# Part of group 1's B/C and of group 2's x moved into the first phase, four gate pairs moved into the first scan stage

## The chip, the cores and the metric

One core of one Trainium2 chip. The metric is device time in microseconds of one execution, as a median over runs. The core has a matrix engine (TensorE, PE, with its weight loads, PEld), a vector engine (VectorE, DVE), a scalar engine (ScalarE, ACT), GpSimd (POOL), and SyncE (SP), whose queue issues most transfers; transfers run on 16 DMA engines. Each engine executes its own list of instructions in order and waits on semaphores for the others.

## The reference, cut to what matters

One layer of a diffusion backbone: 256 latent tokens x and 256 context tokens ctx, model width 2048.

```python
hx = modulate(rmsnorm(x, norm_mix), sh1, sc1)      # sh1, sc1 from silu(c) @ w_mod + b_mod
proj = h @ w_in                                    # for x and for ctx
z, xbc, dt_raw, glu, gates = split(proj, [4096, 10240, 10368, 14464])
xbc = silu(dwconv_seq(xbc, conv_w, conv_b))        # width 5, centred
xs, bm, cm = split(xbc, [4096, 5120])              # 64 heads of 64; 8 groups of state 128
y = ssd_chunked(forward) + flip(ssd_chunked(flipped)) # x starts from the end states of ctx
y_a = rmsnorm((y + d_skip * xs) * silu(z), ssm_norm) @ w_proj_a
u, v = split(glu, 2); cf = silu(layernorm(cf_conv(u * sigmoid(v))))
g_a, g_b = split(gates, 2)
x = x + g1 * ((sigmoid(g_a) * y_a + sigmoid(g_b) * (cf @ w_proj_b)) @ w_out)
x = x + g2 * swiglu(modulate(rmsnorm(x, norm_ffn), sh2, sc2)) ; out = rmsnorm(x, norm_final)
```

All inputs are float32. The scan of a group needs its own x, B, C and dt; z is needed after the scan; the gates only near the end of the first sub-layer.

## The kernel before, in words

Every large product is made from two float32r halves: a weight tile w (float32, 128 x up to 1024) is cast to wh by ACT (line 114), and DVE makes the rest wl = w - wh (line 115); the activations hx are kept as a high and a low half in the same way. The 512 columns of hx are 256 latent and 256 context tokens. `mm_unit` (132) multiplies one unit of weights: up to four row blocks (128 rows of the model width each, 16 in all) by 256 columns, that is two parts of 128 columns. A wide part (1 in the list `wide`) has three 128x512 matmuls per row block, for latent and context tokens; a narrow part (0) has one 128x512 and one 128x256, for latent tokens alone. A weight tile lives in w32 (6 buffers, filled from SP's queue, line 107), then in wh and wl (4 each). Accumulators are PSUM tiles `acc`, four in all, so two pairs of parts.

**First phase (358 to 517).** The modulation vectors sh1 and sc1 come from 64 units of w_mod that PE multiplies with silu(c) (`mod_units`, 400, line 413), and they are needed before hx of a row block can be made (429 to 440). So the product with w_in starts before hx is complete: the row blocks are taken in blocks (`BLOCKS`), and for each block a list of `pairs` of columns is multiplied: dt, the x tiles of groups 0 and 1 (four x pairs of 256 columns) and B and C of group 0. The partial sums are added in SBUF after each block (line 509). Between the pairs of one block stand the mod_units of the next block. With the last block the sums are complete: they get the conv and SiLU (`conv`, 279: ACT, four DVE taps, ACT), and `dt_chain` (301) makes the decay tables in small steps and sends cs_d and ec_d to DRAM.

**Scan stages 1 to 8 (796 to 824).** Stage s runs the scan of group s-1 (`ssd`, 584, a generator with 15 steps) between units of w_in: `bcpair` (B and C of group s), `xpair` (x of group s+1), `zpair` (z of an earlier group) and, in stages 7 and 8, `gpair`: five of the 16 gate pairs (256 columns of gates each), which are kept in SBUF in the x tiles' buffers (tag xc, 9 buffers) in the list `early`. Each unit has a nominal duration; `beg` and `end` bound the stretch over which the scan's steps are spread.

**After the scan.** At 826 the gate tiles ga and gb are allocated and the early gates get their sigmoid (832). Then come the GLU pairs (873 to 892), then the remaining gate pairs with the layernorm between them (`layernorm`, 894, nine steps; 922 to 934), then w_proj_b, w_proj_a, w_out, and the FFN. Between their units a `hook` runs steps of `modvec` (519), which reads the other columns of w_mod; `bg(mgen, 108, 226)` sets 108 steps over 226 units.

**What sets the order.** The Python order gives priorities; the list of each engine is fixed when the program is built, by a planner with a cost model that takes the first instruction in this order that is ready by its reckoning. `tc.high_priority(offset=HP)` moves casts, splits and the first phase's additions ahead by 450. A tile of a tag with n buffers waits until the last reader of the tile n before it is done. POOL issues the transfers of `yg_d`, `cs_d` and `ec_d` from its own queue.

## Time and profile before

| | us |
|---|---|
| median of 3 runs (lowest, highest) | 2398.35 (2396.97, 2398.81) |
| the profiled execution's own time | 2399.29 |
| its span, first to last instruction | 2397.6 |
| PE busy | 2337.8 (98%) |
| DVE busy | 1633.7 (68%) |
| ACT busy | 1252.8 (52%) |
| POOL busy | 126.9 (5%) |

The span is cut into stretches from the beginning of the span, given as 30 to 63 us and so on. "Busy" is time in which an instruction of the engine runs; matmuls overlap, so PE's busy time is read with the waits and with the distance from one matmul's start to the next. The granted clock is the share of the 2.4 GHz that TensorE was given. A wait is put down to the semaphore that came last.

### The profile page before, as it was taken

How to read it: one execution, taken by the hardware profiler on the slowest of the kernel's cores; microseconds unless marked ns; L12 is line 12 of the kernel's file. 1: busy time of each engine (PE TensorE's matmuls, PEld its weight loads, DVE VectorE, ACT ScalarE, POOL GpSimd, SP SyncE). 2: the span in 40 equal slices, each digit the busy share in tenths (PEclk: the TensorE clock that was granted, in tenths of full speed). 3: DMA queues.
4: the chain of work that ended last, by engine and by line, in shares of the span. 5: the costliest groups of instructions: out<-in, count | busy, mean ns of one | idle time of the engine just before them, and what ended most of it. 6: DMA issues, size and time to landing. Idle time of an engine off the chain costs nothing.

```text
span 2397.6 us, 34659 instructions
## 1 busy us (share of the span) xinstructions
PE 2337.8 (98%) x13180; PEld 1968.7 (82%) x13180; DVE 1633.7 (68%) x2099; ACT 1252.8 (52%) x1934; POOL 126.9 (5%) x149
## 2 busy tenths in 40 slices
PE   6899999999999999999999999998999999999998
PEld 3668788888888788888888888888888888888888
DVE  4559867676676776889878776767666566655554
ACT  4335766666566675654575444445444444444433
POOL 1000000100000000011300000000000000000000
PEclk9999999999999999999999999999999999999999
DMA  9884545546455566888799987885777677767553
GB/s 276 273 272 135 134 133 150 159 134 159 131 150 162 147 189 192 280 254 284 227 286 300 287 275 249 299 289 169 224 230 222 214 226 225 227 201 247 194 193 115
DMA packets 444848, 510.46 MB, mean 213 GB/s; under 512 B 17944, under 2 KB 391927, under 8 KB 443529
## 3 DMA queue, kind: packets, MB, share of 16 engines
q1 hardware_dynamic: 438904, 488.75, 66.7%
q0 software_dynamic: 5216, 18.41, 2.2%
q8 instruction: 103, 1.69, 0.3%
q10 hardware_dynamic: 560, 1.08, 0.1%
q14 instruction: 65, 0.52, 0.1%
HBM read 499.51 MB, written 8.67 MB: 212 GB/s over the span
## 4 chain that ended last, share of the span: by engine, by line
PE 89%; DMA 5%; DVE 2%; ACT 2%; issue 1%; SPq 1%; DVEq 0%; ACTq 0%
PE acc L152 34%; PE acc L154 18%; PE acc L144 6%; PE acc L145 5%; PE acc L147 5%; PE acc L177 4%; PE acc L174 4%; PE acc L175 4%; DMA w<-in_w_mod_dram 3%; PE acc L156 2%; DMA w<-in_w_in_dram 2%; PE ss L716 1%; PE ss L413 1%; DMA cs<-cs_d 1%; PE ss L686 1%
## 5 line engine op out<-in xcount | busy, mean ns | idle before, releaser
L115 DVE TENSOR_TENSOR wl<-w,wh 128x1024 fp32r<-128x1024 f32 (+3 forms) x702 | 847.1, 1210 | 486.6 <-ACT wh L114 484.4
L114 ACT CAST wh<-w 128x1024 fp32r<-128x1024 f32 (+3 forms) x702 | 717.7, 1024 | 742.2 <-PE acc L152 349.6
L152 PE MATMUL acc<-hx,wh 128*128 128x512 f32 x1556 | 433.0, 397 | 0.0
L152 PE MATMUL acc<-h,wh 128*128 128x512 f32 x1290 | 356.6, 395 | 1.9 <-DVE fe L204 1.9
L152 PEld LDWEIGHTS acc<-hx,wh 128*128 128x128 f32 x1556 | 271.9, 189 | 40.8 <-issue 2.2
L154 PEld LDWEIGHTS acc<-hx,wl 128*128 128x128 f32 x1664 | 254.8, 188 | 37.6 <-DVE wl L115 2.1
L144 PE MATMUL acc<-hx,wh 128*128 128x512 f32 x656 | 266.3, 407 | 3.0 <-ACT wh L114 2.6
L154 PE MATMUL acc<-hx,wl 128*128 128x256 f32 x1664 | 265.1, 281 | 1.4 <-DVE wl L115 1.4
L145 PE MATMUL acc<-hx,wh 128*128 128x512 f32 x656 | 259.2, 395 | 0.2 <-DVE hx L440 0.2
L152 PEld LDWEIGHTS acc<-h,wh 128*128 128x128 f32 x1290 | 225.5, 189 | 34.0 <-DVE fe L204 2.6
L154 PEld LDWEIGHTS acc<-h,wl 128*128 128x128 f32 x1376 | 211.5, 189 | 29.7
L537 DVE SCALAR_TENSOR_TENSOR mac<-w,silc,mac 128x1024 f32<-128x1024 f32 x120 | 154.7, 1289 | 104.7 <-DMA w<-in_w_mod_dram 104.0
L154 PE MATMUL acc<-h,wl 128*128 128x256 f32 x1376 | 219.5, 281 | 0.0
L147 PE MATMUL acc<-hx,wl 128*128 128x512 f32 x656 | 183.2, 392 | 0.0
L144 PEld LDWEIGHTS acc<-hx,wh 128*128 128x128 f32 x656 | 124.2, 189 | 38.1 <-ACT wh L114 8.2
L175 PE MATMUL acc<-wh,hid 128*128 128x512 f32 (+1 forms) x440 | 146.8, 347 | 0.0
L174 PE MATMUL acc<-wh,hid 128*128 128x512 f32 (+1 forms) x440 | 146.8, 347 | 0.0
L145 PEld LDWEIGHTS acc<-hx,wh 128*128 128x128 f32 x656 | 124.3, 190 | 26.3 <-issue 1.4
L147 PEld LDWEIGHTS acc<-hx,wl 128*128 128x128 f32 x656 | 123.3, 188 | 27.2 <-issue 0.7
L152 PE MATMUL acc<-yg,wh 128*128 128x512 f32 x496 | 136.3, 395 | 0.0
L177 PE MATMUL acc<-wl,hid 128*128 128x512 f32 (+1 forms) x440 | 109.5, 347 | 0.0
L667 ACT ACTIVATE cs<-cs,ncs 128x128 f32<-128x128 f32 x256 | 81.6, 390 | 34.6 <-DMA cs<-cs_d 30.9
(331 smaller groups left out, 2795.0 us busy)
## 6 DMA issues: line engine op xcount, KB each, us to landing
w<-in_w_in_dram SPq DMA_DIRECT2D x248, 512.0 KB, 4.5
w<-in_w_mod_dram SPq DMA_DIRECT2D x192, 512.0 KB, 4.8
w<-in_w_ffn_gate_dram SPq DMA_DIRECT2D x88, 512.0 KB, 4.5
w<-in_w_ffn_up_dram SPq DMA_DIRECT2D x88, 512.0 KB, 4.5
w<-in_w_ffn_down_dram SPq DMA_DIRECT2D x88, 512.0 KB, 3.7
w<-in_w_proj_a_dram SPq DMA_DIRECT2D x64, 512.0 KB, 5.0
w<-in_w_in_dram SPq DMA_DIRECT2D x74, 256.0 KB, 3.8
cs<-cs_d SPq DMA_DIRECT2D x32, 512.0 KB, 5.8
```

The costliest lines, as they stand in the source:

```text
L114: A.copy(out=hi[:, :n], in_=t[:, :n])
L115: V.tensor_tensor(out=lo[:, :n], in0=t[:, :n], in1=hi[:, :n].bitcast(F32), op=ALU.subtract)
L144: E.matmul(o, wj(hi, k), act(kofs + k)[:, 0, :ncol], start=kofs + k == kbeg, stop=False)
L145: E.matmul(o, wj(hi, k), act(kofs + k)[:, 1, :ncol], start=False, stop=False)
L147: E.matmul(o, wj(lo, k), act(kofs + k)[:, 0, :ncol], start=False, stop=last and k == nk - 1)
L152: E.matmul(o2, wj(hi, k), act(kofs + k)[:, :, :T], start=kofs + k == kbeg, stop=False)
L154: E.matmul(o[:, :T], wj(lo, k), act(kofs + k)[:, 0, :T], start=False, stop=last and not hold)
L174: E.matmul(o, act(kofs + k)[:, 0, s], hi[:, k], start=kofs + k == 0, stop=False)
L175: E.matmul(o, act(kofs + k)[:, 1, s], hi[:, k], start=False, stop=False)
L177: E.matmul(o, act(kofs + k)[:, 0, s], lo[:, k], start=False, stop=kofs + k == kend - 1)
L537: V.scalar_tensor_tensor(out=ac, in0=wt, scalar=silc[:, k - 1:k], in1=ac, op0=ALU.mult, op1=ALU.add)
L667: A.activation(out=t4[:, r, j], in_=t4[:, r, j], func=AF.Identity, bias=ncs[:, cc, r * 64 + hs + j:r * 64 + hs + j + 1])
```

## The change

Seven blocks become eight: 1, 1, 2, 2, 2, 2, 2, 4. In all blocks but the last the list of pairs has two more: B and C of group 1, and the first x pair of group 2. So after row block 11 their sums stand in SBUF (Bt1, Ct1, xts0[8:10]); the last four row blocks of both follow in scan stage 1, as one unit each, and are added to the sums there. Stage 1 has a new order: the one unit of group 2's first x pair, all of its second x pair, gate pair 0, the one unit of B/C of group 1, gate pairs 1 to 3. The scan's steps start from 20 instead of 8 in nominal time. Stage 7 has gate pair 4, stage 8 gate pairs 5 to 8, so nine instead of five gate pairs are early. An early gate is folded into the tile `sz` (one buffer, which `zpair` and `bcpair` use too) and sent to a DRAM tile eg_d from POOL's queue; it is read back into ga and gb after the scan, and its sigmoid stands after the GLU pairs. Seven gate pairs are left for the stretch of the layernorm, whose nine steps are dealt out as 0, 2, 2, 2, 1, 1, 1; 210 takes the place of 226 in the hook. To make room, xc has 10 buffers, the scan's temporary y shares btok's buffer, and `sta` shares a buffer of h32.

```diff
-BLOCKS = (1, 1, 2, 2, 2, 4, 4)
+BLOCKS = (1, 1, 2, 2, 2, 2, 2, 4)
...
+    eg_d = dpool.tile([P, 2 * KD, T], F32, name="eg_d")
...
-        return pa1.tile([P, 512], F32, tag="xc", name="xc", bufs=9)
+        return pa1.tile([P, 512], F32, tag="xc", name="xc", bufs=10)
...
-        sta = p0.tile([P, 2 * P], F32, name="sta")
+        sta = p0.tile([P, 512], F32, tag="h32", name="h32", bufs=3)
...
-                 ([(OFF_Z + 512, 256)], xts0[4:6], [1, 1]), ([(OFF_Z + 768, 256)], xts0[6:8], [1, 1])]
+                 ([(OFF_Z + 512, 256)], xts0[4:6], [1, 1]), ([(OFF_Z + 768, 256)], xts0[6:8], [1, 1]),
+                 ([(OFF_B + P, P), (OFF_C + P, P)], [Bt1, Ct1], [1, 0]),
+                 ([(OFF_Z + 1024, 256)], xts0[8:10], [1, 1])]
...
+            if last:
+                pairs = pairs[:6]
...
-                    t = ptile([P, 4, P], "y")
+                    t = ptile([P, 4, P], "btok")
...
-        def xpair(g, j):
+        def xpair(g, j, sums=None):
             a = acc2()
-            for k0 in range(0, KD, UK):
+            kb = KD - BLOCKS[-1] if sums else 0
+            for k0 in range(kb, KD, UK):
                 hi, lo = unit_cols(w_in, k0, UK, [(OFF_Z + g * 512 + j * 256, 256)])
-                mm_unit(a, hi, lo, UK, k0, KD, [1, 1], hxa)
+                mm_unit(a, hi, lo, UK, k0, KD, [1, 1], hxa, kbeg=kb)
                 yield
             for i in range(2):
-                xt_[g].append(conv(a[i], 512, g * 4 + 2 * j + i, xct()))
+                o = sums[i] if sums else xct()
+                if sums:
+                    V.tensor_tensor(out=a[i], in0=o, in1=a[i], op=ALU.add)
+                xt_[g].append(conv(a[i], 512, g * 4 + 2 * j + i, o))
...
-            early.append(fold(a, xct().rearrange("p (i t) -> p i t", i=2)))
+            t = fold(a, ptile([P, 2, T], "sz", 1))
+            nc.gpsimd.dma_start(out=eg_d[:, 2 * j:2 * j + 2, :], in_=t)
+            early.append(j)
...
-            gs_ = [(gpair(j), 2.56) for j in {7: [0], 8: [1, 2, 3, 4]}.get(stage, [])]
+            gs_ = [(gpair(j), 2.56) for j in {1: [0, 1, 2, 3], 7: [4], 8: [5, 6, 7, 8]}.get(stage, [])]
...
+            if stage == 1:
+                tasks = [(xpair(2, 0, begun["x"]), 5.12)] + xs_ + gs_[:1] + [(bcpair(1, begun["bc"]), 3.84)] + gs_[1:]
...
-            beg = 8 if stage == 1 else 0
+            beg = 20 if stage == 1 else 0
...
-    for j, t in enumerate(early):
-        A.activation(out=ga[:, 2 * j:2 * j + 2, :], in_=t, func=AF.Sigmoid)
     pas.close()
+    gate = [(ga, gb)[j // 8][:, 2 * (j % 8):2 * (j % 8) + 2, :] for j in range(16)]
+    for j in early:
+        nc.gpsimd.dma_start(out=gate[j], in_=eg_d[:, 2 * j:2 * j + 2, :])
...
-    hook = bg(mgen, 108, 226)
+    hook = bg(mgen, 108, 210)
...
+        for j in early:
+            A.activation(out=gate[j], in_=gate[j], func=AF.Sigmoid)
+        for k in range(0, KD, 2):
+            t = ga[:, k:k + 2, :]
+            V.tensor_tensor(out=t, in0=t, in1=rsta.unsqueeze(1).to_broadcast([P, 2, T]), op=ALU.mult)
+        for j in range(len(early), 16):
+            fold(pair(w_in, OFF_GLU + j * 256, KD, hxa, hook), gate[j])
+            A.activation(out=gate[j], in_=gate[j], func=AF.Sigmoid)
+            for _ in range((0, 2, 2, 2, 1, 1, 1)[j - len(early)]):
+                next(ln, None)
```

`bcpair` is changed as `xpair` is: one unit, then the sums are added to both accumulators ahead of the conv.

## Rows read from the trace of the kernel before

**Rows 1.** The page of the whole execution: its head line, and the busy time of TensorE (PE) in us, its share of the span and its count of instructions.

```profile
span 2397.6 us, 34659 instructions
...
PE 2337.8 (98%) x13180; PEld 1968.7 (82%) x13180; DVE 1633.7 (68%) x2099; ACT 1252.8 (52%) x1934; POOL 126.9 (5%) x149
```

**Rows 2.** Who PE waited for, over the whole span: line and tile of the waiting instruction, what it waited for, and then us in total, times, longest wait in us.

```profile
PE ss L413 <- DMA w<-in_w_mod_dram: 20.3, 12, 12.3
...
PE acc L144 <- ACT wh L114: 2.6, 6, 0.8
...
PE acc L152 <- DVE cfx L945: 2.6, 1, 2.6
...
PE tp L420 <- ACT ev L417: 2.0, 3, 1.0
...
PE acc L154 <- DVE wl L115: 1.4, 1, 1.4
...
PE tp L432 <- DVE sc L421: 0.4, 1, 0.4
```

**Rows 3.** Busy us of each engine, block by block, in the first phase and the first scan stage (columns: stretch, its length, then for PE, weight loads PEld, DVE, ACT and POOL the busy us with the count of instructions, then the granted clock of PE as a share of full speed, the busy share of the DMA engines, and GB/s). The stretches are: row blocks 0 and 1; 2 and 3; 4 and 5; 6 and 7; 8 to 11; 12 to 15 (the last block of the first phase); scan stage 1.

```profile
30.00:63.00 33.00, 29.34 (x237) 17.53 (x235) 18.88 (x44) 14.93 (x36) 0.00 (x0) 1.00 0.92 280
63.00:83.30 20.30, 20.08 (x128) 14.64 (x128) 15.39 (x29) 7.53 (x15) 0.00 (x0) 1.00 0.90 278
83.30:106.00 22.70, 21.91 (x164) 15.52 (x160) 13.21 (x27) 6.25 (x12) 0.00 (x0) 1.00 0.79 237
106.00:142.40 36.40, 31.13 (x228) 20.84 (x224) 19.14 (x38) 9.95 (x19) 0.00 (x0) 0.91 0.87 275
142.40:187.00 44.60, 42.02 (x261) 31.04 (x257) 23.51 (x38) 14.82 (x22) 0.00 (x0) 0.96 0.95 287
187.00:215.60 28.60, 28.60 (x129) 23.75 (x128) 26.68 (x36) 17.13 (x22) 0.00 (x0) 1.00 0.40 113
215.60:302.00 86.40, 84.59 (x433) 66.80 (x432) 78.44 (x119) 60.44 (x119) 5.65 (x6) 1.00 0.48 126
```

**Rows 4.** Who PE waited for between 30 and 187 us, the longest in total (columns as in rows 2; the lines L144, L420 and L432 of rows 2 stand in this answer too, with the same totals).

```profile
PE ss L413 <- DMA w<-in_w_mod_dram: 6.8, 9, 1.6
```

**Rows 5.** PE's timeline at two places in the first phase (start us, duration us, engine, line, operation, output and inputs, shape, count): the first matmul of a slow run of w_in matmuls and the instruction behind that run, and the same a second time.

```profile
116.56 0.78 PE L144 MATMUL acc<-hx,wh 128*128 128x512 f32 x1
...
121.27 0.49 PE L432 MATMUL tp<-ident,xt 128*128 128x128 f32 x3
...
152.52 0.78 PE L144 MATMUL acc<-hx,wh 128*128 128x512 f32 x1
...
154.76 0.39 PE L145 MATMUL acc<-hx,wh 128*128 128x512 f32 x1
```

**Rows 6.** PE's timeline in the first phase (columns as in rows 5): begin and end of the B/C pair over row blocks 4 and 5 (95.03 to 97.22), of an x pair over the same two (101.35 to 104.17), of the B/C pair over row blocks 12 to 15 (200.60 to 204.70) and of an x pair over the same four (210.16 to 215.60).

```profile
95.03 0.50 PE L144 MATMUL acc<-hx,wh 128*128 128x512 f32 x1 [0.79 <-ACT wh L114]
...
97.22 0.40 PE L144 MATMUL acc<-hx,wh 128*128 128x512 f32 x1
...
101.35 0.40 PE L144 MATMUL acc<-hx,wh 128*128 128x512 f32 x1
...
104.17 1.93 PE L413 MATMUL ss<-w,sil 128*32 128x256 f32 x32
...
200.60 0.39 PE L144 MATMUL acc<-hx,wh 128*128 128x512 f32 x1
...
204.70 0.40 PE L144 MATMUL acc<-hx,wh 128*128 128x512 f32 x1
...
210.16 0.39 PE L144 MATMUL acc<-hx,wh 128*128 128x512 f32 x1
...
215.60 0.39 PE L144 MATMUL acc<-hx,wh 128*128 128x512 f32 x1
```

**Rows 7.** What SP's DMA queue waited for between 30 and 187 us, the longest in total (columns as in rows 2).

```profile
SPq L107 <- PE ss L413: 55.4, 37, 5.7
```

**Rows 8.** DVE's timeline at the start: the copy that makes rb, and the first instruction that reads it.

```profile
25.68 0.69 DVE L463 COPY rb<-tp 128x512 f32<-128x512 f32 x1 [0.99 <-PE tp L462]
...
30.47 0.69 DVE L434 TENSOR_TENSOR h<-tp,rb 128x512 f32<-128x512 f32 x1
```

**Rows 9.** Scan stage 1: in DVE's timeline the four taps of one x tile's conv, and the first tap of the B tile of group 1; and line 607, the transposes of the x tiles of group 0 on PE (count, duration in ns as min/median/max, first and last start in us).

```profile
249.85 2.72 DVE L289 SCALAR_TENSOR_TENSOR xc<-xt,vt,xc 128x510 f32<-128x510 f32 x4
252.50 0.74 DVE L289 SCALAR_TENSOR_TENSOR Bt<-acc,vt,Bt 128x508 f32<-128x508 f32 x1
...
L607 PE MATMUL tp<-ident,xc x16: 270/272/273, 245.6 to 260.6; 128*128 128x128 f32 x16
```

**Rows 10.** PE's timeline in the GLU phase: the begin of one unit of a gate or GLU pair (four row blocks, 256 columns), and the begin of the next unit.

```profile
1005.77 1.09 PE L152 MATMUL acc<-hx,wh 128*128 128x512 f32 x4
...
1008.57 1.09 PE L152 MATMUL acc<-hx,wh 128*128 128x512 f32 x4
```

**Rows 11.** The transfers of 256 KB between SBUF and the DRAM tile yg_d, issued from POOL's queue: us from issue to landing.

```profile
DMA to landing us min/median/max: 2.5/4.2/6.6
```

**Rows 12.** Busy us in the GLU pairs (960 to 1140) and in the gate pairs with the layernorm (1140 to 1265), columns as in rows 3; and the layernorm's last step, line 917 on ACT (first and last start in us).

```profile
960.00:1140.00 180.00, 180.00 (x1032) 156.94 (x1031) 157.78 (x226) 97.29 (x131) 21.95 (x16) 1.00 0.86 273
1140.00:1265.00 125.00, 123.61 (x708) 107.09 (x706) 102.61 (x117) 80.70 (x111) 20.78 (x19) 1.00 0.82 259
...
L917 ACT ACTIVATE cf<-cf,vt x16: 588/602/616, 1220.6 to 1244.6; 128x256 f32<-128x256 f32 x16
```

More of the change, by code (lines that the diff above doesn't have):

```diff
@@ L364, in _block @@
             V.tensor_tensor(out=sel, in0=sel, in1=ident[:, 32 * j:32 * j + 2], op=ALU.add)
-        sta = p0.tile([P, 2 * P], F32, name="sta")
+        sta = p0.tile([P, 512], F32, tag="h32", name="h32", bufs=3)
         stb = p0.tile([P, 512], F32, tag="ev", name="ev", bufs=2)
-        st = [sta[:, :P]] + [stb[:, i * P:(i + 1) * P] for i in range(4)] + [sta[:, P:]]
+        st = [sta[:, :P]] + [stb[:, i * P:(i + 1) * P] for i in range(4)] + [sta[:, P:2 * P]]
         if vecs.n % P:
@@ L468, in _block @@
         dt_raw = p0.tile([P, 512], F32, name="dt_raw")
-        xts0 = [xct() for _ in range(8)]
-        Bt0, Ct0 = bt(), ct()
+        xts0 = [xct() for _ in range(10)]
+        Bt0, Ct0, Bt1, Ct1 = bt(), ct(), bt(), ct()
         pairs = [([(OFF_XBC, P)], [dt_raw], [1]),
@@ L779, in bcpair @@
             V.tensor_tensor(out=a[1][:, :T], in0=ctl[:, 0], in1=a[1][:, :T], op=ALU.add)
-            bc_[g] = (B_, conv(a[1][:, :T], T, 40 + g, ct()))
+            if sums:
+                V.tensor_tensor(out=a[0], in0=B_, in1=a[0], op=ALU.add)
+                V.tensor_tensor(out=a[1][:, :T], in0=C_, in1=a[1][:, :T], op=ALU.add)
+            bc_[g] = (conv(a[0], 512, 32 + g, B_), conv(a[1][:, :T], T, 40 + g, C_))
         xt_ = {g: [] for g in range(G)}
@@ L784, in _block @@
         bc_ = {0: (Bt0, Ct0)}
+        begun = {"x": xts0[8:10], "bc": (Bt1, Ct1)}
         yr = {g: [] for g in range(G)}
@@ L806, in _block @@
             sg = ssd(stage - 1, xt_[stage - 1], *bc_[stage - 1], yr[stage - 1])
-            durs = [d for _, d in tasks for _ in range(KD // UK)]
-            beg = 8 if stage == 1 else 0
+            nu = [1 if stage == 1 and n in (0, 3) else KD // UK for n in range(len(tasks))]
+            durs = [d for (_, d), m in zip(tasks, nu) for _ in range(m)]
+            beg = 20 if stage == 1 else 0
             end = (sum(durs) if stage < G else sum(durs[:-8])) - 3
@@ L811, in _block @@
             for n, (tk, d) in enumerate(tasks):
-                for _ in range(KD // UK):
+                for _ in range(nu[n]):
                     next(tk)
@@ L922, in _block @@
         ln = layernorm()
-        for j in range(16):
-            t, o = (ga, gb)[j // 8], j % 8
-            t = t[:, 2 * o:2 * o + 2, :]
-            if j >= len(early):
-                fold(pair(w_in, OFF_GLU + j * 256, KD, hxa, hook), t)
-                A.activation(out=t, in_=t, func=AF.Sigmoid)
-                if j > len(early):
-                    next(ln, None)
-            if j < 8:
-                V.tensor_tensor(out=t, in0=t, in1=rsta.unsqueeze(1).to_broadcast([P, 2, T]), op=ALU.mult)
+        for j in early:
[8 more added lines that the diff above has]
+                next(ln, None)
         for _ in ln:
```

15 lines of the change are left out of this document (8 added, 7 removed).

## The prediction, written before the result was known

> **What bounds the kernel now.** I read the page first: PE is busy for 2337.8 of 2397.6 us [rows 1], so in the whole run only 59.8 us are without a matmul, and a change that leaves PE's work alone can win nothing but part of these. The view of waits says where they are [rows 2]: the largest sum, 20.3 us, is PE waiting for w_mod tiles (12.3 of it one wait at the start, before any work is there). Then I cut the first phase and scan stage 1 by blocks [rows 3]. Between 30 and 187 us PE is short of work in some blocks and not in others: row blocks 2 and 3 lose 0.2 us of 20.3, row blocks 6 and 7 lose 5.3 of 36.4, and in these the granted clock falls to 0.91 (1.2 instead of 2.4 GHz for a part of the time). From 187 us PE is busy throughout, and DVE is what is nearly full: 26.68 + 78.44 = 105.1 of 115 us until 302. So the first phase has gaps in PE and stage 1 has none to speak of (86.40 - 84.59 = 1.8 us). The change takes work out of the second and puts it into the first.
>
> **The prize.** Waits of PE from 30 to 187 us: 6.8 us for w_mod [rows 4], and the 2.6, 2.0 and 0.4 us for wh, ev and sc, which lie in the same stretch [rows 2, 4]: 11.8 us. Slow clock: the twelve w_in matmuls from 116.56 to 121.27 us took 4.71 us [rows 5]; the same twelve of an x pair over two row blocks took 104.17 - 101.35 = 2.82 [rows 6]; 1.9 lost. Five matmuls from 152.52 to 154.76 took 2.24 against 5/12 x 2.82 = 1.18; 1.1 lost. Both falls follow PE's waits. Together 11.8 + 1.9 + 1.1 = 14.8 us.
>
> **What moves, and its price.** Twelve row blocks of one B/C pair and one x pair. In blocks of two they cost PE 97.22 - 95.03 = 2.19 and 2.82 us, six times: 30.1 us (the two single blocks priced as one of two). In stage 1 they cost three units each of 204.70 - 200.60 = 4.10 and 215.60 - 210.16 = 5.44 us [rows 6]: 28.6 us go. Net +1.4 us, from the start of more and shorter groups. Splitting row blocks 8 to 11 into two blocks makes six more groups of this kind at (2.82 - 5.44/2) to (2.19 - 4.10/2), 0.10 to 0.14 us: +0.7. Sum **+2.1 us** (ends 1.4 and 3).
>
> **How much of the prize is taken.** Per block of two rows the transfers are 8 w_mod tiles of 524 KB and 1408 columns x 256 rows x 4 bytes = 5.64 MB. Row blocks 2 and 3 moved 278 GB/s at a share of 0.90 [rows 3], so 309 at full share: 18.2 us, under the 20.3 that PE took. With the 512 new columns 6.16 MB, 19.9 us, against 20.3 + 5.0 = 25.3 of PE. PE is then the bound by 5 us a block, and no gap should stay. The worst stretch, 18 steps of w_mod in one block of two, comes once in both versions, with row blocks 6 and 7 now (36.4 - 5.3 idle - 1.9 of slow clock = 29.2 us of work) and with row blocks 10 and 11 then: work 29.2 + 5.0 = 34.2, transfers 8.39 + 1.97 MB = 33.5 us, even, and SP comes into it with its buffers full: what it waits for most, 55.4 us, is that PE's w_mod matmuls give up a tile [rows 7]. In row blocks 0 and 1, idle 33 - 29.34 = 3.7 us, new work of 5 us meets 1.05 MB (3.4 us) of new transfers. I leave 1.5 us there and 1.5 in the last crowded block: **3.0 us stay** (ends 0, and 10 if the DMA engines, at shares of 0.79 to 0.95, give no more). The additions that the new pairs need lie on DVE, three of 128x512 and one of 128x256 per block, beside 15.39 of 20.30 us busy: room is there; were it gone, the accumulators would be late by one addition, 0.7 us a block (the copy of that shape in [rows 8]).
>
> **Start.** The third of the four scale tiles in h32 now waits until sta has been transposed. rb is made at 25.68 + 0.69 = 26.4 us and first read at 30.47 [rows 8]: 4 us of room. I take **0.5** (ends 0 and 2).
>
> **Stage 1.** The four gate pairs are 16 units at 1008.57 - 1005.77 = 2.80 us [rows 10], 44.8 us in stage 1 and 44.8 gone from the gate stretch: nothing net. They bring DVE slack, because in the GLU pairs, with a conv and modvec beside the same unit, it is 157.78 of 180 busy [rows 12]. What can be late is this: xts0 holds all ten xc buffers, so the conv of group 2's second x pair waits until the scan has transposed the x tiles of group 0, and holds two of the four accumulators until then. Now these transposes end at 260.6 + 0.3, 73.9 us after the last block's start [rows 9]; DVE is full until then, with B1's conv beginning at 252.50. In the new order the second x pair ends 28.6 + 5.4 + 21.8 = 55.8 us after that start, gate 0 at 67, B/C's one unit at 71. Gate 0 and B/C share the other two accumulators; gate 1 has to wait for B/C's conv (four taps take 2.72 us [rows 9], and the ACT step ahead of them) or for the x pair's, which ends 73.9 + 2 x 2.72 + some 1.5 (my estimate for ACT) = 81. So PE may stand for 0 to 10 us, and 14 if the two convs of the first x pair, now ahead of the scan, delay the transposes by as much (2 x 2.72) again. At the other end stage 1's own 1.8 us of idle vanish. dt_chain's and the scan's matmuls fill part of any gap, and two accumulators go on turning, so I take **+2.0** (ends -1.8 and 14).
>
> **Waits that are added elsewhere.** sz is busy until its transfer has landed, 4.2 us in the median, 6.6 at most for the same size and queue [rows 11]. Behind gate 0 the next writer is B/C's ACT copy, one unit (4.1 us) later: up to 2.5 us on ACT, with the fold and casts behind it; casts are placed ahead by priority and PE has up to four split units, 11 us, in hand. All other writers come 11 us later. 0 us (ends 0 and 1). y in btok's buffer puts the next group's btok copy behind the last addition of y, which the order of the steps asks for anyway: 0 (ends 0 and 2). The nine read-backs, 2.36 MB, wait on POOL's queue for sz's memory and delay only POOL's later sums; at 273/0.86 = 317 GB/s they are 7.4 us of transfers in a stretch of 180 us that has 14% = 25 us free [rows 12]. The hook's 108/210 for 108/226 steps per unit adds 0.037 x 524 KB per 2.80 us, 7 GB/s to 273. 0 (ends 0 and 3).
>
> **Gate stretch.** 125 - 44.8 = 80 us hold seven pairs and the whole layernorm. DVE was busy 102.61 there [rows 12]; four pairs at no more than a GLU pair's 157.78/16 = 9.9 take away up to 39, so at least 63 stay, and perhaps 72, of 80. The last step's ACT work took from 1220.6 to 1244.6 [rows 12]; dealt out twice as fast it should end some 5 us before the last gate pair. If not, w_proj_b's first wait, 2.6 us now [rows 2], grows by up to 4. The 1.4 us for wl [rows 2], the only idle time in this stretch, may stay or go. 0 (ends -1.4 and 4).
>
> **Sum.** -14.8 + 3.0 + 2.1 + 0.5 + 2.0 = -7.2 us. The profiled execution took 2399.29, 0.94 above the median of the runs shown, so 2392.1 for it, and **2391.1** for the median.
>
> A page's rule would give another result. In row blocks 2 and 3 PE idles 0.2 us of 20.3 while PEld is busy 14.64, 72%; in the last block 23.75 of 28.60, 83% [rows 3]. The Trainium skill, page Perfetto Trace Analysis, section Identifying the Most-Contended Engine, says that matmul busy time hides headroom and that the share of weight loading shows it. By that the 99.6 us of PEld from 30 to 187 us are 120 us at 83%, 37 us would be free, all 28.6 us taken out of stage 1 would be won, and the time would be 2369.7. The 72% without a wait speak against it: the w_mod matmuls load little and stream much.
>
> **The rivals.**
> 1. *Slower: the accumulators in stage 1.* At its upper end the wait behind gate 0 or B/C is 14 us instead of 2: 2391.1 + 12 = 2403. It decides where PE stands there for more than 9.2 us, which is what the other terms win. For it: DVE full, all xc buffers held, two more convs ahead of the scan. Against: gate 0 was put in between, and two accumulators turn.
> 2. *No gain: the first phase stays bound by transfers.* 10 of 14.8 us stay: 2391.1 + 7 = 2398. For it: shares up to 0.95 and 287 GB/s. Against: row blocks 2 and 3 at 0.90 lost nothing, and SP waits for buffers, not for bandwidth.
> 3. *More: nothing stays.* No gap in the first phase, no cost in stage 1, its 1.8 us gone: -14.8 + 2.1 - 1.8 = -14.5, 2384.
> 4. *The reading of the weight loads:* 2369.7.
>
> **How the numbers follow.** Forecast 0.46 (its own range 2387.5 to 2394.5), rival 1 0.13, rival 2 0.18, rival 3 0.20, rival 4 0.03. 0.2% is 4.8 us, about what a measurement can tell: faster is below 2393.6, slower above 2403.1. Faster: 0.42 of the forecast, 0.20, 0.03, and 0.03 of rival 2: 0.68. Same: 0.04, 0.13, and 0.04 of rival 1: 0.21. Slower: 0.09 of rival 1 and 0.02 where rival 2 meets the upper ends of the later terms: 0.11. The range goes from 2383, just below rival 3, to 2401, short of rival 1.
>
> **What would show it.** Right: PE's waits for w_mod after 30 us fall from 6.8 to under 3, the first phase without the last block ends near 187 + 30.1 + 0.7 + 0.5 - 11.8 = 206 to 207 us, and its clock is at 0.98 or more throughout; stage 1 begins near 235 and lasts some 86.4 - 28.6 + 44.8 + 2 = 105 us; the gate stretch is 45 us shorter. Wrong: the last block begins after 212 (rival 2); PE shows a wait of more than 5 us between the second x pair's and gate 1's matmuls (rival 1); PE's first wait in w_proj_b is over 5 us; or gaps come up in the GLU pairs at the read-back.

## The result, and the profile after the change

The changed kernel took **2422.48 us** (median of 4 runs, 2420.02 to 2424.79) against 2397.66 for the kernel before (4 runs): ratio 1.0102, 95% interval 1.0086 to 1.0119. It is slower by 24.8 us where 7.2 less had been forecast, and lies outside the range. The page of its profiled execution (which took 2421.70 us; columns as in rows 1) says:

```profile
span 2419.9 us, 34862 instructions
...
PE 2343.3 (97%) x13180; PEld 1970.9 (81%) x13180; DVE 1655.9 (68%) x2160; ACT 1250.5 (52%) x1956; POOL 131.9 (5%) x167
```

Against [rows 1] the matmuls are as many; PE is busy 5.5 us longer, and idle 16.8 longer (76.6 against 59.8). The 5.5 us hold the shorter groups of the first phase (2.1 by the prediction's prices) and the lower clock that the windows below show. Who PE waited for over the whole span, as in [rows 2]:

```profile
PE ss L414 <- DMA w<-in_w_mod_dram: 15.5, 5, 12.2
PE tp L612 <- ACT btok L634: 10.3, 2, 9.5
PE tp L862 <- POOL var L927: 6.5, 1, 6.5
...
PE acc L153 <- DVE cfx L965: 4.9, 1, 4.9
...
PE acc L153 <- ACT wh L115: 1.5, 1, 1.5
```

The w_mod waits behind the first fell from 20.3 - 12.3 = 8.0 to 3.3. From 30 us to the last block (203.3), the stretch of which the prediction spoke, they are now

```profile
PE ss L414 <- DMA w<-in_w_mod_dram: 2.1, 2, 1.5
```

against 6.8 before [rows 4]; "under 3" had been forecast. Two waits are new: 9.5 us for btok, a tile of the scan, and 6.5 for var, a tile of the layernorm. The windows (columns as in rows 3) place them. In order they are the first phase, its last block, 111 us from the start of stage 1, the 60 us around the wait for btok, the worst ten of these, the GLU pairs, the gate pairs, and the worst twenty of these.

```profile
30.00:203.30 173.30, 168.03 (x1115) 119.52 (x1116) 115.91 (x226) 63.72 (x132) 0.00 (x0) 0.99 0.84 256
203.30:232.00 28.70, 28.70 (x130) 23.77 (x129) 25.57 (x35) 16.44 (x23) 0.00 (x0) 1.00 0.57 169
232.00:343.00 111.00, 97.48 (x531) 79.37 (x530) 97.11 (x149) 70.24 (x133) 9.05 (x9) 0.94 0.52 143
220.00:280.00 60.00, 48.66 (x232) 39.16 (x231) 58.61 (x94) 30.23 (x46) 1.49 (x2) 0.90 0.39 106
270.00:280.00 10.00, 3.47 (x8) 2.14 (x9) 10.00 (x16) 7.03 (x17) 0.00 (x0) 0.50 0.59 133
1009.00:1189.00 180.00, 176.54 (x998) 151.20 (x997) 156.95 (x226) 93.07 (x129) 20.49 (x25) 1.00 0.87 280
1189.00:1282.00 93.00, 81.56 (x460) 70.35 (x458) 80.74 (x95) 64.84 (x93) 27.23 (x21) 0.96 0.82 261
1230.00:1250.00 20.00, 13.46 (x70) 11.41 (x69) 17.63 (x16) 10.25 (x13) 10.73 (x7) 0.83 0.86 269
```

The first phase is full as hoped (5.3 us idle of 173.3; before, 12.5 of 157 [rows 3]). From 220 to 280 us DVE is busy 58.61 of 60 while PE idles 11.3, and at its end the granted clock is 0.50, that is 1.2 GHz.

To see what each part won or lost I cut the profiled executions at five events that all kernels have. From each difference to the kernel before I take the PE work that was moved in or out of the stretch, by the prices of the prediction. The stretches are **F** to the last input transposes of the first phase (180.3 us before), **S1** from there to the first sum of squares (yss) in stage 2, **S2-8** to the last yss, **G** to the first matmul with cfx (the layernorm's output in two halves, which w_proj_b reads), **R** to the first matmul with hid (the FFN's inner activations), behind which nothing differs by more than 1 us. The change moves +30.8, +16.2, 0, -44.8 and 0 us of PE work. The table gives us lost against the kernel before (minus: won).

| kernel | F | S1 | S2-8 | G | R | median us |
|---|---|---|---|---|---|---|
| changed kernel | -14.6 | +14.3 | -2.5 | +14.1 | +8.1 | 2422.5 |
| first-phase part alone | -10.5 | +21.3 | -3.0 | +2.2 | +5.9 | 2416.7 |
| gate part alone | -6.9 | -1.8 | -0.3 | +14.3 | +8.9 | 2415.5 |
| taps left out | -12.9 | +0.8 | -2.3 | +15.2 | +7.5 | 2410.8 |
| squares added on PE | -10.4 | +13.4 | -1.7 | +9.7 | +5.5 | 2417.7 |
| no modvec in gate pairs | -12.7 | +14.1 | -3.2 | +5.9 | +3.7 | 2409.8 |
| B/C alone begun | -13.2 | 0.0 | -2.9 | +15.0 | +5.2 | 2407.1 |
| B/C alone, one gate | -9.6 | +5.5 | -2.8 | +4.9 | +5.6 | 2407.8 |
| B/C alone, no modvec in gates | -12.6 | +2.1 | -2.4 | +10.4 | +4.5 | 2398.0 |
| the same, squares on PE too | -10.6 | +0.4 | -2.5 | +11.4 | +0.3 | 2399.2 |
| before, start edit only | +0.3 | -0.3 | -2.5 | +0.8 | +6.6 | 2395.9 |
| before, taps left out | -1.6 | +0.8 | -1.5 | -0.3 | +6.6 | 2400.0 |
| before, no modvec in gates | -4.8 | +0.3 | -2.8 | +0.2 | +0.3 | 2395.0 |

The row of the start edit shows how far single executions scatter: its code is that of the kernel before from the first block on, and it has -2.5 and +6.6 in S2-8 and R. (That execution took 2404.1 us, its median is 2395.9.) The control without taps shows nearly the same two numbers. So the one execution of the kernel before against which the table counts seems to have been quick in R and slow in S2-8 by its own chance, and most of the +8.1 in R is likely not the change's. F scatters too: with the old first phase it ended at 173.4 to 180.6 us in five executions, 177.7 in the mean, where the table counts from 180.3. So I read S1 and G, F with some 3 us of doubt, and treat R as mostly chance.

### The profile page after: what moved, and what is told of

It reads as the page before. It is cut to its first block, busy times and chain, and to the rows that moved or that the text cites. A ratio compares the mean times of both kernels' runs of the same rounds, so it can differ in the third digit from the quotient of the medians.

```text
span 2419.9 us, 34862 instructions
## 1 busy us (share of the span) xinstructions
PE 2343.3 (97%) x13180; PEld 1970.9 (81%) x13180; DVE 1655.9 (68%) x2160; ACT 1250.5 (52%) x1956; POOL 131.9 (5%) x167
## 3 DMA queue, kind: packets, MB, share of 16 engines
q10 hardware_dynamic: 560, 1.08, 0.1%
## 4 chain that ended last, share of the span: by engine, by line
PE 75%; DMA 4%; DVE 4%; issue 2%; ACT 1%; POOL 1%; DVEq 0%; SPq 0%; ACTq 0%; POOLq 0%
PE acc L153 29%; PE acc L155 15%; PE acc L178 4%; PE acc L176 4%; PE acc L175 4%; PE acc L145 4%; PE acc L146 4%; PE acc L148 4%; DMA w<-in_w_mod_dram 3%; PE acc L157 2%; DVE wl L116 2%; PE ss L721 1%; POOL var L927 1%; DVE mac L542 1%; PE ss L691 1%
## 5 line engine op out<-in xcount | busy, mean ns | idle before, releaser
L116 DVE TENSOR_TENSOR wl<-w,wh 128x1024 fp32r<-128x1024 f32 (+3 forms) x716 | 849.4, 1190 | 493.5 <-ACT wh L115 491.0
L153 PE MATMUL acc<-hx,wh 128*128 128x512 f32 x1550 | 435.4, 399 | 1.5 <-ACT wh L115 1.5
L153 PE MATMUL acc<-h,wh 128*128 128x512 f32 x1290 | 356.9, 396 | 2.2 <-DVE fe L205 2.2
L153 PEld LDWEIGHTS acc<-hx,wh 128*128 128x128 f32 x1550 | 271.8, 190 | 44.1 <-issue 3.3
L153 PEld LDWEIGHTS acc<-h,wh 128*128 128x128 f32 x1290 | 225.4, 189 | 34.4 <-DVE fe L205 2.8
L153 PE MATMUL acc<-yg,wh 128*128 128x512 f32 x496 | 136.4, 395 | 0.0
```

The costliest lines, as they stand in the source:

```text
L116: V.tensor_tensor(out=lo[:, :n], in0=t[:, :n], in1=hi[:, :n].bitcast(F32), op=ALU.subtract)
L153: E.matmul(o2, wj(hi, k), act(kofs + k)[:, :, :T], start=kofs + k == kbeg, stop=False)
```

## The experiments

The brackets hold the ratio to the kernel before, which ran beside each group of versions (medians 2397.2 to 2398.9 us), and its 95% interval.

**1. The two halves of the change.** The first has the new BLOCKS, pairs and sums but gates {7: [0], 8: [1, 2, 3, 4]}, the old hook and one layernorm step per pair; the second has the old first phase, full B/C and x pairs, and the four gates behind them. Both begin the scan's steps at 8, as before the change.

```diff
@@ first-phase part alone
-gs_ = [(gpair(j), 2.56) for j in {1: [0, 1, 2, 3], 7: [4], 8: [5, 6, 7, 8]}.get(stage, [])]
+gs_ = [(gpair(j), 2.56) for j in {7: [0], 8: [1, 2, 3, 4]}.get(stage, [])]
@@ gate part alone
-BLOCKS = (1, 1, 2, 2, 2, 2, 2, 4)
+BLOCKS = (1, 1, 2, 2, 2, 4, 4)
-tasks = [(xpair(2, 0, begun["x"]), 5.12)] + xs_ + gs_[:1] + [(bcpair(1, begun["bc"]), 3.84)] + gs_[1:]
+tasks += xs_ + gs_
```

> The first-phase part of the change alone: the row blocks 0 to 11 of B/C of group 1 and of two x tiles of group 2 are still begun there, but no gate pair lies in stage 1 (gates 0 to 4 in stages 7 and 8, eleven gate pairs later, hook and layernorm steps as before the change). Theory D (DVE's backlog: the convs of the last block, dt_chain and the scan's own steps take DVE the same time from the last block's start on, whatever PE does): PE runs out of work in stage 1, the first stage-2 sum of squares comes at 348 to 356 us where PE's work alone would put it at 327 (338.8 before), so the 13 us won in the first phase are lost again and more: 2405 to 2414. Theory O (the 14 us of stage 1 come from the order on PE, because gate units stand behind the scan's transposes): without gate units nothing is held up, 2385 to 2392. Both expect the gate stretch as before the change.

> The gate part of the change alone: the first phase, the full B/C and x pairs of stage 1 and beg = 8 as before the change, with gates 0 to 3 behind them in stage 1, nine gates by way of DRAM, seven gate pairs with the layernorm, hook 108/210. Theory G (the loss behind stage 8 comes from the shorter gate stretch and from the read-back, not from the first phase): between the last yss of stage 8 and the first cfx matmul 10 to 15 us are lost, and the total is 2408 to 2418. Rival (it comes from how the stages fall in time once the first phase is changed, or is chance): the stretch loses under 4 us and the total is 2396 to 2402.

Measured: 2416.74 us (1.0078, 1.0063 to 1.0093) and 2415.49 (1.0078, 1.0056 to 1.0100). Each half alone is slower. With the first-phase part alone the first yss came at 351.8 us, in theory D's range (the total is 2.7 above it), and S1 lost 21.3, which is 7 more than with the gates in it; with the gate part alone S1 lost nothing, and this is the whole list of waits of PE from 205 to 390 us:

```profile
PE tp L610 <- ACT xs L643: 0.8, 1, 0.8
```

But G lost 14.3, the same as in the changed kernel. So the loss of stage 1 belongs to the first-phase part, that of the gate stretch to the gates, and neither to the other.

**2. Stage 1: the order on PE, or DVE's backlog?** What stood on PE in the changed kernel (columns as in rows 5):

```profile
263.45 1.08 PE L148 MATMUL acc<-hx,wl 128*128 128x512 f32 x4
266.39 0.66 PE L612 MATMUL tp<-ident,xc 128*128 128x128 f32 x4 [1.86 <-DVE ncs L347]
276.53 1.12 PE L612 MATMUL tp<-ident,xc 128*128 128x128 f32 x4 [9.48 <-ACT btok L634]
277.44 1.92 PE L639 MATMUL ss<-xw,btok 128*128 128x512 f32 x2
278.93 0.85 PE L153 MATMUL acc<-hx,wh 128*128 128x512 f32 x1
```

After the second x pair (to 264.5) come the scan's transposes, which wait for ACT's copy of btok; gate 0 (L153) stands behind them. The sixteen transposes of the x tiles (as L607 in [rows 9]) end 86.2 us after the last block's start, where they had ended 73.9 us after it:

```profile
L612 PE MATMUL tp<-ident,xc x16: 272/273/477, 266.4 to 289.2; 128*128 128x128 f32 x16
```

On ACT that copy stood behind SiLUs which waited for convs:

```profile
271.80 1.29 ACT L293 ACTIVATE xc<-xc 128x512 f32<-128x512 f32 x2 [4.59 <-DVE xc L290]
...
275.91 0.57 ACT L634 COPY btok<-tp 128x512 f32<-128x512 f32 x1
```

and on DVE the convs of the last block and those of the first x pair follow one another without a gap:

```profile
267.06 5.37 DVE L290 SCALAR_TENSOR_TENSOR xc<-xt,vt,xc 128x508 f32<-128x508 f32 x8
272.33 1.29 DVE L776 TENSOR_TENSOR acc<-xc,acc 128x512 f32<-128x512 f32 x2
...
274.18 5.35 DVE L290 SCALAR_TENSOR_TENSOR xc<-acc,vt,xc 128x508 f32<-128x508 f32 x8
```

The last of these, until 279.5, still read the accumulators (xc<-acc) that gate 0 has to write next. Two locks, then, with one key: DVE. That leaves open whether another order would do. First I began the scan later, then put two gates first, with and without their folds ahead by priority:

```diff
-beg = 20 if stage == 1 else 0
+beg = 30 if stage == 1 else 0
@@ gates first (beg = 34)
+tasks = gs_[:2] + [(xpair(2, 0, begun["x"]), 5.12)] + xs_ + gs_[2:3] + [(bcpair(1, begun["bc"]), 3.84)] + gs_[3:]
@@ folds ahead
+with tc.high_priority(offset=HP):
+    t = fold(a, ptile([P, 2, T], "sz", 1))
```

> The changed kernel with the scan's first step in stage 1 placed after 30 instead of 20 units of planned time, so that gate 0 stands ahead of the scan's transposes on PE. Theory O (order on PE): gate 0 runs in the gap, the wait of 9.5 us for btok falls below 2 us, and 8 to 11 us come back: 2411 to 2415. Theory D (DVE's backlog holds the accumulators of the first x pair as well): the wait only changes its name, from btok to an accumulator behind the convs of xc, first ydiag within 3 us of 311: 2419 to 2425.

> The changed kernel with stage 1 in another order: gates 0 and 1 first, then both x pairs, gate 2, B/C, gate 3, the scan begun after 34 units of planned time, and the gate pairs' folds placed ahead by priority as the casts are, so that their accumulators come free though DVE is behind. Theory D (the wall is DVE's backlog, and work that needs nothing from DVE but casts and a fold fits in front of it): the wait of 9.5 us for btok falls to 0 to 3, the idle time of PE from 250 to 390 us falls from 13.5 to under 6, and 8 to 12 us come back: 2410 to 2415. Rival (the work of stage 1 is bound by DVE's sum, in whatever order): the gap comes back later in the stage, 2419 to 2425.

> The same order without the priority: gate 0's fold stands in DVE's and ACT's list behind the last block's convs. Theory D: gates 0 and 1 fill four accumulators until about 255 us and the x pair then waits for gate 0's fold, behind the backlog, until 268 to 275: the gap stays 8 to 15 us and the time is 2418 to 2428. Rival (order alone counts, not what frees an accumulator): as with the priority, 2410 to 2415.

Measured: 2435.39 us (1.0161, 1.0144 to 1.0178), 2434.54 (1.0157, 1.0126 to 1.0188) and 2431.11 (1.0144, 1.0117 to 1.0171): all worse than the changed kernel by 9 to 13 us, and than any theory had expected. S1 lost 25.2, 24.9 and 22.1. With beg = 30 gate 0 did not come ahead of the transposes on PE, so this run does not put the question: the wait for btok stays, gate 0 starts right behind it again, and a second gap appears where the convs hold an accumulator:

```profile
PE tp L612 <- ACT btok L634: 9.5, 1, 9.5
PE acc L153 <- DVE xc L290: 4.9, 1, 4.9
```

With the gates first and their folds ahead the wait for btok is gone, and PE waits for the fold and for dt_chain instead:

```profile
PE acc L145 <- DVE sz L205: 7.6, 2, 5.4
PE tp L346 <- DVE xt L338: 4.9, 1, 4.9
```

The priority did not help: the first fold's copy came at 276.59 us on ACT, right behind the last of the first phase's convs (sz may lie in memory that the sums in xt held until then; that was not tried), and DVE itself then stood idle for 8.1 us, waiting for ACT's copy of the second fold. So none of the orders tried is better; that none could be is not shown. By count gates are the poorer cover: a gate unit asks DVE for one split (1.22 us) per 2.80 us of PE, an x unit per 5.44.

The direct trial of theory D leaves DVE work out and changes nothing on PE, in the changed kernel and, as a control, in the kernel before:

```diff
-        for tap in (0, 1, 3, 4):
+        for tap in taps:
-4: 4 + j, 5: 6 + j}[i], pt)
+4: 4 + j, 5: 6 + j}[i], pt, (1, 3))
```

> The changed kernel without the two outer taps of the ten convs that follow the first phase's last block (this part of the convolution is left out): some 13 us less of DVE between 225 and 275 us, nothing of PE changed. Theory D (in stage 1 PE stands because DVE is behind with these convs): the wait of 9.5 us for btok and the slow clock after it go, 9 to 13 us come back, 2409 to 2414. Rival (the order on PE or the accumulators' turn, not DVE's load): 2419 to 2424.

> The same taps left out of the kernel before, as a control: there PE loses 1.8 us in stage 1, so both theories expect 2394 to 2399. If it wins 8 us or more, DVE bounds the kernel there already and theory D's gain above says nothing on the change.

Measured: 2410.76 us (1.0049, 1.0034 to 1.0064) and 2399.97 (1.0008, 0.9996 to 1.0021). 11.7 us come back in the one and nothing in the other. The two windows of before, now without those taps:

```profile
220.00:280.00 60.00, 59.69 (x299) 48.42 (x298) 53.44 (x82) 41.47 (x64) 1.49 (x2) 1.00 0.46 127
270.00:280.00 10.00, 10.00 (x57) 8.09 (x56) 5.77 (x9) 9.26 (x18) 0.00 (x0) 1.00 0.59 141
```

PE idles 0.3 instead of 11.3 us, the clock is whole, and S1's loss falls from 14.3 to 0.8: **DVE's backlog is shown as the cause in stage 1.**

**3. Which work covers it.** If x pairs are the cover, then they should stay and B/C alone be begun early:

```diff
-                 ([(OFF_B + P, P), (OFF_C + P, P)], [Bt1, Ct1], [1, 0]),
-                 ([(OFF_Z + 1024, 256)], xts0[8:10], [1, 1])]
+                 ([(OFF_B + P, P), (OFF_C + P, P)], [Bt1, Ct1], [1, 0])]
+tasks = xs_ + gs_[:1] + [(bcpair(1, begun["bc"]), 3.84)] + gs_[1:]
@@ one gate
+gs_ = [(gpair(j), 2.56) for j in {1: [0], 7: [1], 8: [2, 3, 4, 5]}.get(stage, [])]
```

> The changed kernel with B/C of group 1 alone begun in the first phase (13 us instead of 30 us of PE moved); both x pairs of group 2 run whole in stage 1, ahead of the gates and B/C's last unit, all else as changed. Theory D (x pairs load DVE with one split per 5.4 us and are the cover for its backlog; gates with one per 2.8 us are not): stage 1 loses 3 us or less instead of 9 to 14, the first phase wins 4 to 8 instead of 11 to 13, the gate stretch loses its 14 as before: 2406 to 2414. Rival (what is moved out of stage 1 is lost there, of whatever kind): 2416 to 2424.

> B/C alone begun in the first phase, one gate pair instead of four moved to stage 1 in its place (six gates early, ten gate pairs with the layernorm at one step each). By D and C the first phase wins 4 to 8, stage 1 loses up to 3, and the ten pairs are cover enough for the layernorm: 2391 to 2399. Rival (every us taken out of stage 1 is lost there): 2400 to 2406.

Measured: 2407.06 us (1.0038, 1.0019 to 1.0057) and 2407.75 (1.0039, 1.0025 to 1.0053). The first is as D has it: S1 loses 0.0, no wait of PE from 205 to 390 us is longer than 1.7, and F wins 13.2, which was more than expected. The second is not, and it is slower than both ranges: with 11 us of gate as the only substitute S1 lost 5.5, and the ten gate pairs lost 4.9 in G. Stage 1 needs nearly all the PE time it had.

The other way to keep the cover is to begin work of another stage, z pairs of stage 2, in the kernel before (their fold is one tile, added to sz later):

```diff
+zts = [xct() for _ in range(nz)]
+([(256 * i, 256)], [zts[i][:, :T], zts[i][:, T:]], [0, 0])
@@ zpair(0, i), kb = 12
+mm_unit(a, hi, lo, UK, k0, KD, [0, 0], hxa, kbeg=kb)
```

> The kernel before with other work begun in the first phase: row blocks 0 to 11 of the first z pair of group 0 (one folded 128x512 tile of sums, 8.4 us of PE taken out of stage 2), the change's blocks and its start, and no other part of it. Theory D (the gaps of the first phase can be filled, but not with work that covers DVE's backlog in stage 1): stage 1 keeps its cover, stage 2 has DVE to spare (62% busy at 340 to 400 us in the changed kernel), and most of the 8.4 us is won: 2389 to 2394. Rival (the first phase is bound by its transfers, and its gain of 13 us in the changed kernel was lent by stage 1): 2397 to 2402.

> As before with both z pairs of group 0 (16.8 us taken out of stage 2, 17.4 us put in, the same transfers as in the changed kernel). Theory D: 8 to 12 us won, 2386 to 2391, unless stage 2 has too little left for PE. Rival: 2396 to 2403.

Measured: 2397.97 us (0.9996, 0.9984 to 1.0009) and 2402.48 (1.0025, 1.0013 to 1.0037). Both miss theory D's ranges and lie in the rival's. But the rival's reason, that what the first phase gains is lent by stage 1, does not hold for B/C alone (F won 13.2, S1 lost 0.0). With two pairs, from 31 us to its last transposes:

```profile
31.00:196.00 165.00, 153.74 (x1054) 106.00 (x1054) 110.86 (x232) 63.66 (x143) 0.00 (x0) 0.98 0.82 255
```

PE idles 11.3 us here, nearly as before. The transfers are those of the changed kernel (6.16 MB a block), but the PE work that they carry is 17.4 + 0.7 = 18.1 us instead of 30.8: F wins 18.1 - (196.0 - 180.3) = 2.4. With one pair F won 7.2. Up to the first yss, where the first pair's 8.4 us had been taken out, the two kernels then lost 2.8 and 5.1. So the z pairs moved were not free either; that PE work per byte of transfers decides what the first phase gives is likely, but these single executions do not show it.

One part of the change was suspected because the gate part alone, with the old blocks, was 6.9 us early in F:

```diff
-sta = p0.tile([P, 2 * P], F32, name="sta")
+sta = p0.tile([P, 512], F32, tag="h32", name="h32", bufs=3)
```

> The kernel before with one edit of the change alone: sta is the first 256 columns of a tile in h32's ring instead of a tile of its own. In the gates-alone run, whose first phase has the blocks and pairs of before, the last transposes of that phase came at 173.4 instead of 180.3 us and PE's first w_mod matmul at 18.6 instead of 19.6. Theory S (this edit shortens the first phase by some 7 us, so half of the gain there is not the moved work's): 2390 to 2393, last transposes at 173 to 175. Rival (chance of the transfers in that run): 2395 to 2399.

Measured: 2395.88 us (1.0001, 0.9984 to 1.0018), last transposes at 180.6. The 6.9 us were chance.

**4. The gate stretch.** First the same nine layernorm steps, dealt otherwise; then the sum of squares taken off POOL; then modvec taken out of the gate pairs, with the kernel before as a control:

```diff
-for _ in range((0, 2, 2, 2, 1, 1, 1)[j - len(early)]):
+for _ in range((1, 2, 1, 0, 2, 2, 1)[j - len(early)]):
@@ squares on PE (sq in fp32r)
-G_.tensor_tensor(out=var, in0=var, in1=sq[:, i, :], op=ALU.add)
+E.matmul(vb[:, :T], onesr, sq[:, i, :], start=k + i == 0, stop=k + i == KD - 1)
@@ no modvec in the gate pairs
-fold(pair(w_in, OFF_GLU + j * 256, KD, hxa, hook), gate[j])
+fold(pair(w_in, OFF_GLU + j * 256, KD, hxa), gate[j])
-hook = bg(mgen, 108, 210)
+hook = bg(mgen, 108, 182)
```

> The changed kernel with the layernorm's nine steps dealt to the seven gate pairs as (1, 2, 1, 0, 2, 2, 1) instead of (0, 2, 2, 2, 1, 1, 1): a gate pair of free time lies between the last var addition on POOL and the rstd matmul. Theory W (the rstd matmul comes too early in PE's list): its wait of 6.5 us for var falls below 1.5, the slow clock of 1230 to 1250 us goes, and the time falls by 6 to 9 us: 2413 to 2416. Rival V (DVE and ACT are the bound of these 80 us): what is won there is lost at the first cfx matmul, whose wait grows from 4.9 to 10 or more: 2419 to 2424.

> The changed kernel with the layernorm's sum of squares taken off POOL: ACT writes the squares rounded to fp32r, and sixteen matmuls with a matrix of ones add them up in PSUM (some 16 times 0.12 to 0.27 us of PE, 2 to 4 us). Theory C (seven gate pairs are too short a cover for the chain mean, 16 additions on POOL of 22 us, rstd, apply): the wait of 6.5 us for var goes, the first cfx matmul waits under 4 us, and 5 to 9 us come back: 2413 to 2417. Rival V (DVE and ACT bound the stretch): 2420 to 2425.

> The changed kernel with no step of modvec in the seven gate pairs of the layernorm's stretch (they are dealt to the other pairs, 108 over 182 units): 14 multiply-adds of 1.3 us less on DVE there. Theory C (the chain mean, var on POOL, rstd, apply is longer than seven gate pairs, and DVE's other work lengthens it): the wait of 6.5 us for var falls to 3 or less, the 272.9 us from the last yss to the first cfx matmul fall to 264 to 268, 2413 to 2418. Rival (the chain's length does not depend on it, or the read-back is the cost): 2420 to 2425.

> The control: the kernel before with no modvec step in its eleven gate pairs (108 over 182 units in the others). Theory C: its chain already has cover enough (no wait for var there, 2.6 us at the first cfx matmul), so it wins 0 to 3: 2394 to 2398. If it wins more than 5, the gain of that edit in the changed kernel is not the layernorm's chain alone.

Measured: 2423.69 us (1.0109, 1.0094 to 1.0125): dealt otherwise, the wait for var goes, and the one for cfx grows to 13.4. 2417.65 (1.0086, 1.0058 to 1.0115): the wait for var goes, the one for cfx grows to 6.7, and G gets back 4.4 of 14.1. 2409.75 (1.0041, 1.0024 to 1.0058): 12.7 us, more than expected, 8.2 of them in G and 4.4 in R. Its waits from 1010 to 1290 us:

```profile
PE acc L153 <- DVE cfx L965: 3.7, 1, 3.7
PE acc L155 <- DVE wl L116: 1.8, 2, 1.5
PE acc L153 <- ACT wh L115: 1.7, 2, 1.4
PE tp L862 <- POOL var L927: 1.4, 1, 1.4
```

The control: 2394.95 (0.9992, 0.9983 to 1.0001), no difference that these runs can tell, and G there is +0.2. So the 8.2 us in G are gained only where the stretch has been cut; the edit takes load off DVE, so it does not tell the chain's length from DVE's load. The chain itself in the changed kernel, its first subtractions on DVE and var's additions on POOL (line, count: duration in ns min/median/max, first and last start), and these additions without modvec:

```profile
L920 DVE TENSOR_TENSOR cf<-cf,mean x8: 689/1058/1230, 1215.4 to 1226.0; 128x512 f32<-128x512 f32 x8
L927 POOL TENSOR_TENSOR var<-var,f x15: 1066/1587/1610, 1218.8 to 1239.6; 128x256 f32<-128x256 f32 x15
```

```profile
L927 POOL TENSOR_TENSOR var<-var,f x15: 722/1197/1756, 1215.5 to 1235.8; 128x256 f32<-128x256 f32 x15
```

and the last step, on ACT (it is L917 of [rows 12]), in the changed kernel:

```profile
L937 ACT ACTIVATE cf<-cf,vt x16: 587/600/614, 1250.9 to 1275.9; 128x256 f32<-128x256 f32 x16
```

**5. Both edits together.** The edits of parts 3 and 4 together: B/C alone begun, with no modvec in the gate pairs, and the same with the squares on PE too.

> B/C of group 1 alone begun in the first phase (x pairs whole in stage 1) and no modvec step in the seven gate pairs; the sum of squares stays on POOL. If the two mended losses add, from 2407 by some 8 to 12: 2394 to 2399, at or a little under the kernel before. If the layernorm's stretch gives back less beside the steps moved to the GLU pairs: 2400 to 2404.

> The kernel with B/C alone begun, with the sum of squares on PE and without modvec in the gate pairs as well. If D and C hold together, both losses go for the greater part: 2398 to 2406. If the gate stretch is bound otherwise: within 3 us of the kernel with B/C alone begun.

Measured: 2397.99 us (1.0003, 0.9994 to 1.0012) and 2399.19 (1.0008, 0.9996 to 1.0019). Stage 1's loss is mended (+2.1 and +0.4). That of the gate stretch is mended in part alone: G still lost 10.4 and 11.4, where B/C alone had lost 15.0. The time is the kernel before's again because the first phase's gain pays for the rest, and no version tried is faster than it by more than the measurement can tell.

The last of these versions says most about G. Its layernorm takes 47.2 us instead of 61 from the first subtraction to the last SiLU and ends 10.8 us before the last gate matmul, and the sixteen added matmuls take 3.4 us of PE. PE no longer waits for var, but these waits stay between the last yss and the first cfx matmul:

```profile
PE acc L153 <- DVE cfx L964: 5.4, 1, 5.4
PE acc L155 <- DVE wl L116: 3.0, 4, 1.8
PE acc L153 <- ACT wh L115: 2.6, 1, 2.6
```

Those for wl and wh lie in the GLU pairs. So the chain's length is not the whole of G's loss, and what the rest comes from (the read-back of nine gates, DVE's and ACT's load) was not tried apart. With five gates read back, in the first-phase part alone, G lost 2.2.

## Why the prediction was wrong

**Right in the main: the first phase.** The last block began at 203.3 us where 206 to 207 had been forecast, w_mod waits from 30 us on fell to 2.1, the clock is 0.99. From 31 us to the last input transposes, before and after:

```profile
31.00:180.30 149.30, 136.78 (x957) 93.47 (x956) 84.44 (x163) 49.76 (x98) 0.00 (x0) 0.97 0.89 274
31.00:196.50 165.50, 160.90 (x1083) 113.66 (x1083) 108.82 (x214) 58.55 (x124) 0.00 (x0) 0.99 0.83 253
```

PE's idle time fell from 12.5 to 4.6 us. F won 14.6 us in this execution; over the nine profiled kernels with the same first phase its end lies at 196.5 to 200.7, 198.9 in the mean, which is 30.8 - 18.6 = 12.2 us won (the sum had 14.8 - 3.0 - 0.5 = 11.3). Counted from the mean of the five executions with the old first phase (177.7) it is 9.6 us. Rival 2 fell for this mix of work, and so did rival 4, by which all 28.6 us would have been won. With the two z pairs PE stayed idle for 11.3 us, so the gaps do not fill with every work. The start cost 0.3 (start edit alone) where 0.5 had been taken.

**Wrong: "Stage 1 ... +2.0".** It measured +14.3, the upper end. Two steps failed. The first is that the transposes of the x tiles would end 73.9 us after the last block's start, as before [rows 9]: they ended 86.2 us after it. DVE was through with the last block's convs 69.1 us after that start (65.6 before [rows 9]), and then, to 76.2, it did the additions and convs of the first x pair, which I had myself put into its list ahead of the scan. The second is "gate 0 at 67", that "gate 0 and B/C share the other two accumulators", and that "two accumulators go on turning". Gate 0 was to run from 55.8 to 67 us after that start and began 75.6 us after it: the second x pair ended at 61.2, gate 0 needs the accumulators of the first x pair, which its convs read until 76.2, and it stands on PE behind transposes that wait for the same backlog. That rival 1 was the truth of stage 1 I saw as a possibility. Its sign came, a wait of more than 5 us between the second x pair and gate 1; its price (14 us) fits by luck in part, since it was a sum of two delays and the trace has 12.6 us of waits and a slow clock behind them. I took a value next to zero because four accumulators seemed enough to keep PE fed. The deeper slip is older: [rows 3] show DVE at 78.44 of 86.40 us in stage 1 and PE at 84.59, both full. I read the second number as a stage without gaps from which work can be taken. It meant that PE's work there was just enough cover for DVE's: with both x pairs left in place S1 lost 0.0, and less DVE work won nothing in the kernel before.

**Wrong: "Gate stretch. ... 0".** It measured +14.1. I added up DVE's load (at least 63 of 80 us) and found room. But the layernorm is a chain: from the first subtraction at 1215.4 us to the last SiLU at 1276.5 it takes 61 us on DVE, ACT, POOL and PE by turns, and of the seven gate pairs (28 units at 2.80 = 78 us, from 1190 or so) only some 52 are left when it starts. It ended 0.5 us before the last gate matmul. Before, it was dealt over eleven pairs, took 83.3 us and still ended 20 us before that matmul. "It should end some 5 us before the last gate pair" was a guess on its pace; its price if wrong, "up to 4", was one wait (the first in w_proj_b, 4.9 now against 2.6) and left out the wait for var, 6.5, and the slow clock behind it (0.83 in 1230 to 1250). The runs show that the loss comes with the four moved gate pairs and that 8.2 us of it go with modvec's steps (4.6 with B/C alone). How the rest divides between the chain, DVE's and ACT's load and the read-back stays open: with the chain ended 10.8 us early 11.4 us were still lost.

**Wrong: "0" for the GLU pairs.** 180 - 176.54 = 3.5 us of idle time are new there, 1.5 of it for wh at 1027 us, right behind the issue of the read-back (1015.4 to 1020.0), and most of the rest in short waits for wl. It is part of G's 14.1. That the read-back causes it is not shown.

**Open: R.** 8.1 us more between cfx and hid. The same stretch showed +6.6 in two executions whose code there is that of the kernel before (and +6.0 and +6.2 with the z pairs), and +0.3 to +4.5 where modvec was dealt differently. So perhaps some 2 us of it are the change's; this is not settled.

Net work (+2.1) was not measured apart and is taken at its price, 30.8 - 28.6 = 2.2. With it the profiled execution adds up: -14.6 + 14.3 - 2.5 + 14.1 + 8.1 + 2.2, and 0.8 behind R, are the 22.4 us by which it was longer than that of the kernel before (2421.70 against 2399.29). The medians differ by 24.8.

## What to carry to other kernels

Where two engines are full in a stage, PE's work is the cover of the other's: before moving it, ask what the other engine will be doing in that time, and whether what comes in its place loads it less (an x unit wants 1.22 us of DVE in 5.44, a gate unit the same in 2.80). A dependent chain such as a layernorm has to be set, with its length from first to last step, against the PE time that lies beside it; busy time alone showed room here where there was none. And when one edit fills a gap and another drains a cover, run each half alone first: the two halves here cost 19.5 and 18.3 us, and neither showed in the sum of loads. They do not add up to the whole (24.8): with the gates of the one half in it, stage 1 lost 7 us less by the other.

## What the runs showed of the hardware

POOL's additions and DVE's subtractions slow each other: in the changed kernel a subtraction of 128x512 took 0.69 us as POOL had not yet begun and up to 1.23 while it added, and POOL's additions there took 1.07 to 1.61 (0.72 without modvec, where DVE stood idle). The Trainium skill, page GPSIMD Engine Reference, section Specifications, says that GpSimd shares its SBUF interfaces with VectorE and that DVE instructions with two SBUF inputs contend for them; the subtraction has two, and the trace agrees. It cuts both ways in a chain that alternates between the two.

A wait costs PE more than its length. Behind the 9.5 us for btok the granted clock was 0.50: gate 0's first four 128x512 matmuls took 2.13 us, and the next four, with the clock at 0.99, 1.08 (columns as in rows 5).

```profile
278.93 2.13 PE L153 MATMUL acc<-hx,wh 128*128 128x512 f32 x4
...
281.68 1.08 PE L153 MATMUL acc<-hx,wh 128*128 128x512 f32 x4
```

Single executions scatter more than the three of the kernel before had suggested: in 25 runs it took 2392.2 to 2403.2 us, and two stretches with unchanged code moved by 2.5 and 6.6.
